# Decoder block on one core: the shared expert ahead of the routed experts, the residual on VectorE, the expert ranking right behind the router

## The chip, the cores and the metric

The kernel runs on one core of a Trainium2 chip. The metric is the device time of one execution in microseconds (us); the median of three runs before the change is 930.93 us (929.96 to 931.77). All arithmetic is on 32-bit floats; where TensorE multiplies, a number is mostly split into a high and a low part of the type `fp32r`, and three products (high by high, low by high, high by low) are added up.

## What is computed

One decoder layer for 256 tokens of width 1024. Attention and a gated recurrence give `x1`, the residual stream after the first LayerNorm. What follows is what the change touches, cut from the reference:

```
h = x1.reshape(B * S, D)                      # 256 x 1024
idx, gate = route(h, w_router, bias)          # 8 of 64 experts per token
y_moe = routed_experts(h, idx, gate, ...)     # each expert: silu(xb Wg) * (xb Wu), then Wd; ff 256
      + swiglu(h, shared_w_gate, shared_w_up, shared_w_down)   # the shared expert, every token
ple = sigmoid(x1 @ ple_gate_w) * (p @ ple_proj_w)              # the "embedding" term
x = layer_norm(ALPHA * x1 + y_moe + ple)
```

Each expert has 3 MB of weights, so the 64 of them have 192 MB, and the shared expert has 3 MB more.

## The kernel before

A helper `mm` (line 105) records nearly every matmul, so tiles tell more than lines: `pj`, `ah`, `mix` belong to the part before `x1`, `acc` is the sum of the output (four banks, two halves of tokens by two halves of columns), `t` and `g` are the banks of the expert part. `load` (line 83) issues every weight transfer on the queue of SP, in order.

**The ring.** Weights arrive in slots of 128 x 2048 floats (1 MB each), which the function `slot` hands out in turn. There are 17 of them while `x1` is made; the buffer of `x1` joins when `x1` is no longer wanted, and two more when the buffers of the embedding's stage are closed, which makes 20. A transfer into a slot waits until the last reader of what was in it is done, and because SP issues in order, every transfer behind it waits too.

**The stage between `x1` and the experts** (380 to 424 us). TensorE transposes `x1` into `x1h` and `x1l` (high and low part, `xT` for short), forms the router's logits, and multiplies `x1` with the embedding's gate: `dense` (two calls, `gated[0]` and `gated[1]`) takes 8 chunks of weights each, splits a chunk on ScalarE (line 119) and VectorE or GpSimd (line 120) and issues 6 matmuls for it. Beside it VectorE selects the 8 experts of every token and makes `posm`, the place of a token among its expert's tokens. `add_emb` (line 806) splits the gated embedding and adds it to `acc` with an identity matrix.

**The experts.** `units` lists 13 units, each with two passes. In ten of them a pass takes 2 experts with up to 64 tokens each; in three (places 2, 7 and 9 of the list, `SMALL_AT`) a pass takes 4 experts with up to 32 tokens each. The function `experts` issues a pass: the gate and up matmuls (`g<-raw,xe`), the activation, the down matmuls (`g<-raw,hT`), the scatter into `acc`; between them it calls the generators in `steps`, which gather the tokens of the next unit. A pass of 2 experts uses 6 MB of weights, one of 4 uses 12 MB, with nearly the same TensorE time.

**The order of the experts.** The first 8 experts (`FIXED`) have their place in the program. From the ninth on the experts are sorted by their number of tokens: `rank` counts, sorts, rewrites `posm` and `gates2`, and leaves the experts' numbers in `ids` (in the tile `cst`, line 737). SP reads a number with `TENSOR_LOAD` (line 815) before it issues that expert's loads, and the number of rounds (tile `rounds`, line 753) likewise. `rank` is a generator whose four pieces are spread over the first two passes of the experts.

**The shared expert** is a generator too, `shared`, and its pieces are spread over units 4 to 6 (`SHARED_AT` 6). It adds `ALPHA * x1` to `acc` with 12 matmuls by a scaled identity matrix, transposes the split `x1` again (32 transposes of 128 x 128), takes its 3 MB of weights in program order behind the experts' loads, issues 48 matmuls for gate and up and 24 for down, and keeps its splits in ring slots.

The last unit's end is the second LayerNorm (`last_norm`) and the store of the result.

Of the kernel before, what the change touches and what calls it, by code (L numbers as in the profile page):

```python
# [33 lines left out]
SHARED_AT = 6  # L34
FIXED, SMALL, SMALL_AT = 8, 24, (2, 7, 9)
# [3 lines left out]
SLOW, EMB_AT, GATHER_AT = ((0, 1), (0, 1, 2)), 4, (3, 4)  # L39
GU_AT = (5, 6)  # L40
# [18 lines left out]
def tile_block(ctx: ExitStack, tc: tile.TileContext, a, out: bass.AP):  # L59
# [560 lines left out]
    add_slots(pxx, 1, X_AT)  # L620
    lg = bank("t")[:NE, :S]

    def ev_ple(f):
        def ev(i, ps):
            o = emb[i][f]
            act.activation(ps, ps, AF.Sigmoid)
            late(dve.tensor_mul(o, o, ps))
        return ev

    gated = [dense([(raw(a["pleg"][2 * f + n]), 4) for n in range(2)], ev_ple(f),  # L630
                   [acc_bank() if f else bank("g") for _ in range(2)], SLOW[f]) for f in range(2)]
    for kt in range(KT):
        if kt == ROUTER_SPLIT:
            next(gated[0])
        ws = slice(NE * kt, NE * kt + NE)
        mm(lg, wrh[:, ws], x1h[:, kt], start=kt == 0, stop=False)
        mm(lg, wrh[:, ws], x1l[:, kt], start=False, stop=False)
        mm(lg, wrl[:, ws], x1h[:, kt], start=False, stop=kt == KT - 1)
# [55 lines left out]
    ids = cst[0:1, C_TRI:C_TRI + NE].bitcast(I32)  # L694

    def rank():


        t = slot()
        bigger, cnt, front, keys = (t[:, n:n + NE] for n in (0, 64, 128, 192))  # L700
        ranked = t[:, 256:384]
        pg, pgT = (t[:, n:n + 256].rearrange("p (i c) -> p i c", i=2) for n in (384, 640))
        em = t[:, 896:1024].rearrange("p (i e) -> p i e", i=2)
        rones, rcol, top, key = (t[:, n:n + 1] for n in range(1024, 1028))
# [93 lines left out]


    s, xe, steps = unit(0)  # L800
# [40 lines left out]
    w0, gu0 = expert_weights(0, 2), bank("g")  # L841
    for kt in range(KT):
        next(gated[1])
        if kt == EMB_AT:
            add_emb(0)
        if kt in GATHER_AT:
            next(steps)
        if kt in GU_AT:
            n = GU_AT.index(kt)
            gate_up(gu0, (2 * n, 2 * n + 1), xe, 0, w0)  # L850
    fixed["pe"] = False
    add_emb(1)
# [7 lines left out]

    def swiglu(h, ps):
        act.activation(h, ps[:, 0:256], AF.Sigmoid)  # L862
        for n in range(2):
            dve.tensor_mul(h, h, ps[:, 256 * n:256 * n + 256])  # L864
# [56 lines left out]
    def shared():  # L921


        keep = slot(F32R)
        ah, al = keep[:, 0:128], keep[:, 128:256]
        act.activation(ah, ident, CP, scale=ALPHA)
        dve.scalar_tensor_tensor(al, ident, ALPHA, ah.bitcast(F32), op0=OP.mult, op1=OP.subtract)
        for i in range(2):
            for f in range(2):
                for l, r in ((ah, xh), (ah, xl), (al, xh)):  # L930
                    mm(acc[i][f], l, r[:, i, 512 * f:512 * f + 512], start=False, stop=False)
                yield
        keep = slot(F32R)
        hth, htl = keep[:, 0:512], keep[:, 512:1024]
        xT = [slot(F32R).rearrange("p (k t) -> p k t", k=KT) for _ in range(2)]

        def split_into(hi, lo, c):
            act.activation(hi, c, CP)
            dve.tensor_sub(lo, c, hi.bitcast(F32))

        def splits(chunks):
            t = None
            for n, c in enumerate(chunks):
                if n % 2 == 0:
                    t = slot(F32R)
                hi, lo = (t[:, 512 * k:512 * k + 512] for k in (2 * (n % 2), 2 * (n % 2) + 1))
                split_into(hi, lo, c)
                yield hi, lo

        for x, t in zip((xh, xl), xT):  # L950
            for k2 in range(4):
                ps = bank("t", (128, 2, S))
                for k in range(2):
                    kt = 2 * k2 + k
                    for i in range(2):
                        transpose(ps[:, k, 128 * i:128 * i + 128], x[:, i, 128 * kt:128 * kt + 128].bitcast(F32))
                if k2 % 2:
                    act.activation(t[:, 2 * k2:2 * k2 + 2], ps, CP)
                else:
                    dve.tensor_copy(t[:, 2 * k2:2 * k2 + 2], ps)  # L960
                yield
        gu = [raw(a["shgu"][n], ordered=True) for n in range(2)]
        dn = raw(a["shd"], ordered=True)
        ps = [bank("g") for _ in range(2)]
        for kt, (whi, wlo) in enumerate(splits([r[:, 512 * k:512 * k + 512] for r in gu for k in range(4)])):
            for i in range(2):
                hi, lo = (t[:, kt, 128 * i:128 * i + 128] for t in xT)
                mm(ps[i], hi, whi, start=kt == 0, stop=False)
                mm(ps[i], lo, whi, start=False, stop=False)
                mm(ps[i], hi, wlo, start=False, stop=kt == KT - 1)  # L970
        hs = slot().rearrange("p (i c) -> p i c", i=2)
        for i in range(2):
            swiglu(hs[:, i, 0:256], ps[i])
        yield
        hT = bank("t", (128, 2, S))
        for i in range(2):
            for ft in range(2):
                transpose(hT[:, ft, 128 * i:128 * i + 128], hs[:, i, 128 * ft:128 * ft + 128])
        split_into(hth, htl, hT.rearrange("p f t -> p (f t)"))
        ws = splits([dn[:, 512 * k:512 * k + 512] for k in range(4)])  # L980
        for f in range(2):
            yield
            for ft in range(2):
                whi, wlo = next(ws)
                for i in range(2):
                    c = slice(256 * ft + 128 * i, 256 * ft + 128 * i + 128)
                    for l, r in ((hth, whi), (htl, whi), (hth, wlo)):
                        mm(acc[i][f], l[:, c], r, start=False, stop=False)

# [11 lines left out]
    ranking = rank()  # L1001
    for q, (r0, ne) in enumerate(units):
        if q + 1 < len(units):
            if q == 1:
                for _ in ranking:
                    pass
            first = steps
            nxt, xnxt, steps = unit(q + 1)
            fill = (none, steps, steps, none), (none, steps, steps, none)
            if q == SHARED_AT - 2:  # L1010
                sh = shared()
                fill = ((sh, steps, steps, sh),) * 2
            if q == SHARED_AT - 1:
                fill = ((zip(sh, sh), steps, steps, zip(sh, sh)),) * 2
            if q == 0:
                fill = ((list(first) for _ in (0,)), steps, steps, ranking), (ranking, steps, steps, ranking)
# [5 lines left out]
        for pr in range(2):  # L1022
            r = r0 + ne * pr
            last = q + 1 == len(units) and pr == 1
            if q == SHARED_AT and pr == 0:
                for _ in rest:
                    pass
                rest = ()
                next(sh)
                chained = (next(sh) for _ in (next(steps, None),))  # L1030
                fill = (sh, steps, chained, sh), fill[1]
# [214 lines left out]
```

## Time and profile before

| | us |
|---|---|
| median of three runs | 930.93 |
| the profiled execution's own time | 932.01 |
| its span, first to last instruction | 930.2 |
| TensorE busy in it | 873.6 (94%) |
| bytes moved by DMA | 270.84 MB, mean 291 GB/s |

The span is what the trace shows; the execution has 1.8 us more around it. Busy time of TensorE is modelled: matmuls overlap, so a high share does not mean that TensorE was what the end waited for. The chain of waits, followed back from the last instruction, tells that. DMA share 1.00 means that all 16 DMA engines were busy.

### The profile page before, as it was taken

The numbers are of one execution on the slowest core, as the hardware profiler recorded it, in microseconds if no ns is written. First come the engines' busy times: TensorE is split into PE (matmuls) and PEld (weight loads), VectorE is DVE, ScalarE is ACT, GpSimd is POOL, SyncE is SP. The second block draws the span as 40 slices with busy tenths as digits, with TensorE's granted clock in tenths as the row PEclk, the third lists the DMA queues.
The fourth block names the chain that finished last, engine by engine and source line by source line (L and its number), as shares of the span: only waits on it lengthen the run. The fifth ranks groups of instructions, "written<-read, shape, count | busy, mean of one in ns | idle before, by whom it ended". The sixth has DMA issues, their size and how long they took to land.

```text
span 930.2 us, 14043 instructions
## 1 busy us (share of the span) xinstructions
PE 873.6 (94%) x5244; PEld 575.7 (62%) x5244; DVE 381.3 (41%) x808; ACT 328.8 (35%) x657; POOL 169.9 (18%) x219
## 2 busy tenths in 40 slices
PE   9999999999999999799998999999987987799993
PEld 7899897878799998665543444546532432244431
DVE  5555555777966566852211221243110111011216
ACT  6444454576665455542221221242110211011221
POOL 1025354734200002440210110120100110101001
PEclk9999999999999999899999999999998999899997
DMA  9953342534246974547399999984999999999971
GB/s 340 421 219 105 123 136 91 183 106 164 81 170 218 395 304 169 186 168 292 154 422 420 420 420 421 421 352 186 421 421 421 419 421 422 420 421 421 412 315 47
DMA packets 42047, 270.84 MB, mean 291 GB/s; under 512 B 5060, under 2 KB 5188, under 8 KB 12280
## 3 DMA queue, kind: packets, MB, share of 16 engines
q1 hardware_dynamic: 41624, 269.20, 72.7%
q8 instruction: 42, 0.69, 0.3%
q10 hardware_dynamic: 288, 0.52, 0.1%
q14 instruction: 29, 0.24, 0.1%
q0 software_dynamic: 64, 0.20, 0.1%
HBM read 268.85 MB, written 1.05 MB: 290 GB/s over the span
## 4 chain that ended last, share of the span: by engine, by line
PE 65%; DMA 27%; DVE 5%; issue 1%; ACT 1%; SPq 1%; DVEq 0%; ACTq 0%
DMA raw<-in_exp_dram 27%; PE pj L105 25%; PE g L105 18%; PE acc L105 5%; PE t L105 5%; PE ah L105 4%; PE mix L474 2%; PE sc L105 1%; PE yp L105 1%; PE ap L383 1%; PE t L108 1%; PE pt L262 1%; DVE hr L367 1%; PE op L105 1%; SPq L83 0%
## 5 line engine op out<-in xcount | busy, mean ns | idle before, releaser
L105 PE MATMUL g<-raw,xe 128*64 128x512 f32 (+1 forms) x1024 | 212.0, 629 | 23.4 <-DMA raw<-in_exp_dram 23.4
L119 ACT ACTIVATE wh<-raw 128x512 fp32r<-128x512 f32 x213 | 132.3, 630 | 121.3 <-PE pj L105 88.1
L120 DVE TENSOR_TENSOR wl<-raw,wh 128x512 fp32r<-128x512 f32 x184 | 129.6, 715 | 90.5 <-ACT wh L119 69.5
L105 PEld LDWEIGHTS g<-raw,xe 128*64 128x64 f32 (+1 forms) x1024 | 61.5, 131 | 154.4 <-issue 110.4
L105 PE MATMUL pj<-xhi,wh 128*128 128x256 f32 x448 | 128.8, 288 | 0.2 <-DVE hq L368 0.2
L105 PE MATMUL pj<-xlo,wh 128*128 128x256 f32 x448 | 128.2, 286 | 0.0
L105 PE MATMUL pj<-xhi,wl 128*128 128x256 f32 x448 | 128.0, 286 | 0.0
L764 POOL TENSOR_SCALAR sel<-cst,posm 128x64 fp32r<-128x64 f32 (+1 forms) x120 | 48.2, 429 | 396.6 <-PE t L105 350.4
L864 DVE TENSOR_TENSOR h<-h,g 128x256 f32<-128x256 f32 x52 | 21.9, 420 | 222.8 <-ACT h L862 221.9
L105 PE MATMUL g<-raw,hT 128*64 128x512 f32 (+1 forms) x512 | 99.5, 598 | 4.3 <-DMA raw<-in_exp_dram 3.8
L862 ACT ACTIVATE h<-g 128x256 f32<-128x256 f32 x26 | 10.0, 384 | 222.5 <-PE g L105 222.5
L105 PEld LDWEIGHTS pj<-xhi,wh 128*128 128x128 f32 x448 | 85.5, 191 | 3.5 <-issue 1.9
L105 PEld LDWEIGHTS pj<-xhi,wl 128*128 128x128 f32 x448 | 85.5, 191 | 3.1 <-issue 2.7
L105 PEld LDWEIGHTS pj<-xlo,wh 128*128 128x128 f32 x448 | 85.5, 191 | 2.7 <-issue 2.4
L908 DVE SCALAR_TENSOR_TENSOR yl<-g,gsl,yh 128x512 fp32r<-128x512 f32 x52 | 39.0, 750 | 116.9 <-ACT yh L907 116.9
L105 PEld LDWEIGHTS g<-raw,hT 128*64 128x64 f32 (+1 forms) x512 | 27.8, 126 | 57.3 <-issue 43.8
L907 ACT ACTIVATE yh<-g,gsl 128x512 fp32r<-128x512 f32 x52 | 35.7, 687 | 75.5 <-PE g L105 75.5
L105 PE MATMUL t<-sel,xh 128*128 128x256 f32 x208 | 56.9, 306 | 1.3 <-DVE gsl L888 1.3
L105 PEld LDWEIGHTS t<-sel,xh 128*128 128x128 f32 x208 | 40.1, 193 | 23.0 <-issue 21.9
L778 ACT ACTIVATE xe<-t 128x512 f32<-128x512 f32 x52 | 31.1, 597 | 64.6 <-PE t L105 64.6
L105 PE MATMUL t<-sel,xl 128*128 128x256 f32 x208 | 52.5, 285 | 0.0
L120 POOL TENSOR_TENSOR wl<-raw,wh 128x512 fp32r<-128x512 f32 x29 | 38.4, 1333 | 60.0 <-ACT wh L119 43.6
(296 smaller groups left out, 1313.7 us busy)
## 6 DMA issues: line engine op xcount, KB each, us to landing
raw<-in_exp_dram SPq DMA_DIRECT2D x180, 1024.0 KB, 19.8
raw<-in_win_dram SPq DMA_DIRECT2D x40, 1024.0 KB, 5.0
raw<-in_exp_dram SPq DMA_DIRECT2D x24, 512.0 KB, 10.1
raw<-in_wab_dram SPq DMA_DIRECT2D x8, 768.0 KB, 5.3
raw<-in_wo_dram SPq DMA_DIRECT2D x4, 1024.0 KB, 8.1
raw<-in_pleg_dram SPq DMA_DIRECT2D x4, 1024.0 KB, 10.5
raw<-in_win_dram SPq DMA_DIRECT2D x8, 256.0 KB, 6.0
raw<-in_shgu_dram SPq DMA_DIRECT2D x2, 1024.0 KB, 19.9
```

Of the source, the lines that this page charges most:

```text
L105: pinned(pe.matmul(o, l, r, start=start, stop=stop))
L108: pinned(pe.transpose(o, t, ident))
L119: act.activation(hi, src, CP)
L120: (lo_engine or dve).tensor_sub(lo, src, hi.bitcast(F32))
L262: pe.transpose(pt[:, b], pr[:, 128 * b:128 * b + 128], ident)
L474: ins = pe.matmul(mix[i][f], l[:, ts], r[f], start=j == n == 0, stop=j == 7 and n == 2)
L764: by.tensor_scalar(s[:, i, w * e:w * e + w], iota[:, 0:w], pos_of(i)[:, e:e + 1], None, op0=OP.is_equal)
L778: act.activation(xe[k2], ps, CP)
L862: act.activation(h, ps[:, 0:256], AF.Sigmoid)
L864: dve.tensor_mul(h, h, ps[:, 256 * n:256 * n + 256])
L907: act.activation(yh, y, CP, scale=gsl)
L908: dve.scalar_tensor_tensor(yl, y, gsl, yh.bitcast(F32), op0=OP.mult, op1=OP.subtract)
```

## The change

- **Shared expert.** `shared` and its 32 transposes go. Its gate and up product is now a third call of `dense`, on the embedding's `x1h` and `x1l`, right behind `gated[1]`; its down product stands between the two halves of the first gate and up matmuls of the first experts. Its weights are asked for right behind the embedding's gate weights, before any expert's. Its splits use the buffers of the embedding's stage and no ring slots.
- **Residual.** `ALPHA * x1` is added to the embedding term on VectorE (4 instructions of 128 x 512), and so reaches `acc` with `add_emb`; the 12 matmuls go.
- **Ranking.** The four pieces of `rank` run between the chunks 1, 2, 3 and 5 of `gated[1]`; its scratch moves from a ring slot to buffers of its own.
- The gather of the first unit moves behind the shared gate and up product; the second small unit moves from place 7 to place 6 of the list.

```diff
-SHARED_AT = 6
-FIXED, SMALL, SMALL_AT = 8, 24, (2, 7, 9)
+FIXED, SMALL, SMALL_AT = 8, 24, (2, 6, 9)
-SLOW, EMB_AT, GATHER_AT = ((0, 1), (0, 1, 2)), 4, (3, 4)
-GU_AT = (5, 6)
+SLOW, RANK_AT = ((0, 1), (0, 1, 2), ()), (1, 2, 3, 5)
...
             late(dve.tensor_mul(o, o, ps))
+            late(dve.scalar_tensor_tensor(o, x1[:, i, 512 * f:512 * f + 512], ALPHA, o, op0=OP.mult, op1=OP.add))
...
+    sh_gu = [(raw(a["shgu"][n]), 4) for n in range(2)]
+    sh_dn = raw(a["shd"])
...
-    w0, gu0 = expert_weights(0, 2), bank("g")
+    w0 = expert_weights(0, 2)
+    ranking = rank()
     for kt in range(KT):
         next(gated[1])
-        if kt == EMB_AT:
+        if kt in RANK_AT:
+            next(ranking)
+    add_slots(pxx, 1, X_AT)
+    s, xe, steps = unit(0)
...
+    shared = dense(sh_gu, ev_shared, [bank("g") for _ in range(2)], SLOW[2])
+    for kt in range(KT):
+        if kt == 2:
             add_emb(0)
-        if kt in GATHER_AT:
-            next(steps)
-        if kt in GU_AT:
-            n = GU_AT.index(kt)
-            gate_up(gu0, (2 * n, 2 * n + 1), xe, 0, w0)
+            hs = ptg.tile([128, 2, S], F32, name="tg", bufs=4)
+        if kt == 4:
+            add_emb(1)
+        next(shared)
+    next(steps)
+    next(steps)
+    hT = bank("t", (128, 2, S))
...
+    act.activation(hth, hTf, CP)
+    late(dve.tensor_sub(htl, hTf, hth.bitcast(F32)))
+    gu0 = bank("g")
+    gate_up(gu0, range(2), xe, 0, w0)
+    for f in range(2):
+        for ft in range(2):
+            n = 2 * f + ft
+            whi, wlo = split(pbd, sh_dn[:, 512 * n:512 * n + 512], 512, "w2", W2)
+            for i in range(2):
+                c = slice(256 * ft + 128 * i, 256 * ft + 128 * i + 128)
+                for l, r in ((hth, whi), (htl, whi), (hth, wlo)):
+                    mm(acc[i][f], l[:, c], r, start=False, stop=False)
+    gate_up(gu0, range(2, 4), xe, 0, w0)
     fixed["pe"] = False
-    add_emb(1)
...
-    def shared():
...
```

How the instructions stand, at three places. First the queue of SP between the embedding's gate weights (`pleg`) and the first expert whose number is read (`cst`); `shgu` and `shd` are the shared expert's weights. Before:

```order
L83 DMA raw<-in_pleg_dram 128x2048 x4
L83 DMA raw<-in_exp_dram 128x2048 x10
L83 DMA xs<-in_rbias_dram 128x64
L83 DMA raw<-in_exp_dram 128x2048 x14
L815 TENSOR_LOAD cst
```

Now:

```order
L81 DMA raw<-in_pleg_dram 128x2048 x4
L81 DMA raw<-in_shgu_dram 128x2048 x2
L81 DMA raw<-in_exp_dram 128x2048
L81 DMA raw<-in_shd_dram 128x2048
L81 DMA raw<-in_exp_dram 128x2048 x7
L81 DMA xs<-in_rbias_dram 128x64
L81 DMA raw<-in_exp_dram 128x2048 x8
L819 TENSOR_LOAD cst
L819 ISA x2
L1029 TENSOR_LOAD rounds
L1029 ISA x2
L81 DMA raw<-in_exp_dram 128x2048 x2
```

The three shared chunks have moved ahead of the experts, and SP reads the numbers and the rounds behind 16 expert chunks instead of 24 (the `cst` pair stands four times in a row).

Second, TensorE where `rank` begins (its first piece has 4 small matmuls). Before, in the first pass of the experts:

```order
L105 MATMUL g<-raw,hT 64x512 x8
L105 MATMUL t<-raw 128x64 x2
L105 MATMUL t<-raw 64x1 x2
L105 MATMUL acc<-yh,sT 128x512
```

Now, in `gated[1]`, behind its second chunk:

```order
L103 MATMUL acc<-w2l,x1h 128x512
L103 MATMUL t<-xs,rcols 128x64 x2
L103 MATMUL t<-rcols,xs 64x1 x2
L103 MATMUL acc<-w2h,x1h 128x512
L103 MATMUL acc<-w2h,x1l 128x512
```

The first piece has moved ahead of six of the eight chunks of `gated[1]`, and all of `rank` ahead of the experts.

Third, TensorE from the end of the shared gate and up product to the shared down product, now (rows that repeat are left out; `tg` is the shared expert's activation, `w2h` and `w2l` its split weights):

```order
L103 MATMUL g<-w2l,x1h 128x512
L103 MATMUL t<-sel_4748,xh 128x256
...
L106 MATMUL t<-cst,tg 128x128 x4
L103 MATMUL g<-raw,xe 64x512 x4
L103 MATMUL acc<-w2h,tg 128x512 x2
L103 MATMUL acc<-w2l,tg 128x512
...
L103 MATMUL g<-raw,xe 64x512 x4
L103 MATMUL t<-sel_4748,xh 128x256
```

Before, the shared products stood in the sixth unit as rows like these:

```order
L105 MATMUL g<-raw 128x512 x48
L105 MATMUL t<-sel_6372,xh 128x256
L105 MATMUL g<-raw,xe 64x512 x8
L105 MATMUL t<-cst,raw 128x128 x4
L105 MATMUL acc<-raw 128x512 x12
```

What stood between passes of the experts now stands before the first one: 24 down matmuls lie between two groups of 4 gate and up matmuls.

## Rows read from the trace of the kernel before

**Rows 1.** The page: DMA share in 40 slices, and the chain that ended last.

```profile
DMA  9953342534246974547399999984999999999971
...
PE 65%; DMA 27%; DVE 5%; issue 1%; ACT 1%; SPq 1%; DVEq 0%; ACTq 0%
DMA raw<-in_exp_dram 27%; PE pj L105 25%; PE g L105 18%; PE acc L105 5%; PE t L105 5%; PE ah L105 4%; PE mix L474 2%; PE sc L105 1%; PE yp L105 1%; PE ap L383 1%; PE t L108 1%; PE pt L262 1%; DVE hr L367 1%; PE op L105 1%; SPq L83 0%
```

**Rows 2.** Busy time by stretch; the last three numbers are granted clock, DMA share, GB/s.

```profile
420.00:424.00 4.00, 4.00 (x21) 3.56 (x21) 0.07 (x1) 0.77 (x2) 0.00 (x0) 0.63 1.01 426
442.00:455.00 13.00, 13.00 (x72) 7.19 (x70) 4.50 (x14) 3.79 (x8) 0.88 (x3) 1.00 0.00 2
...
606.00:642.00 36.00, 34.71 (x176) 21.80 (x176) 13.80 (x27) 13.07 (x25) 5.32 (x16) 1.00 0.55 223
642.00:823.00 181.00, 155.82 (x846) 66.52 (x844) 27.30 (x67) 25.84 (x49) 15.26 (x40) 0.96 1.01 421
...
904.00:930.00 26.00, 10.23 (x46) 4.23 (x42) 14.29 (x36) 4.56 (x8) 4.18 (x3) 0.77 0.11 42
```

**Rows 3.** Waits on SP's queue, 380 to 930 us: total, times, longest.

```profile
SPq L815 <- DVE cst L737: 16.7, 1, 16.7
```

**Rows 4.** Issues on SP's queue, in order of time: start, length, what.

```profile
455.09 0.97 SPq L83 DMA_DIRECT2D raw<-in_exp_dram  x2
...
893.85 0.33 SPq L83 DMA_DIRECT2D raw<-in_exp_dram  x1
```

**Rows 5.** The page, DMA issues: KB each, median us to landing.

```profile
raw<-in_exp_dram SPq DMA_DIRECT2D x24, 512.0 KB, 10.1
```

**Rows 6.** The chain of waits, 528 to 570 us: start, length, what.

```profile
533.77 1.03 PE acc L105 x4
...
547.76 1.15 PE t L105 x8
...
549.25 1.03 PE acc L105 x4
...
565.78 1.03 PE acc L105 x4
```

**Rows 7.** The chain of waits, 383 to 430 us.

```profile
399.22 5.61 PE acc L105 x24
...
415.76 0.91 PE acc L105 x3
...
419.40 1.56 PE acc L105 x3
...
423.79 3.58 PE g L105 x16
```

**Rows 8.** VectorE in order of time, 399 to 406 us.

```profile
401.58 1.41 DVE L764 TENSOR_SCALAR sel<-cst,posm 128x64 fp32r<-128x64 f32 x8
...
403.52 0.21 DVE L706 TENSOR_SCALAR raw<-posm 128x128 f32<-128x128 f32 x1
```

**Rows 9.** Line 512 on VectorE: durations min/median/max in ns.

```profile
L512 DVE SCALAR_TENSOR_TENSOR x<-x,st,raw x4: 737/1242/1829, 376.4 to 380.5; 128x512 f32<-128x512 f32 x4
```

**Rows 10.** GpSimd's splits, 383 to 405 us: count, busy, mean ns, idle before.

```profile
L120 POOL TENSOR_TENSOR w2l<-raw,w2h 128x512 fp32r<-128x512 f32 x3 | 3.9, 1306 | 7.7 <-ACT w2h L119 7.7
```

**Rows 11.** TensorE in order of time: the 4 matmuls of `rank`'s first piece (8 records).

```profile
434.64 0.98 PE L105 MATMUL t<-raw 128*128 128x64 f32 x8
```

**Rows 12.** The page, costliest groups: busy us, mean ns, idle before.

```profile
L119 ACT ACTIVATE wh<-raw 128x512 fp32r<-128x512 f32 x213 | 132.3, 630 | 121.3 <-PE pj L105 88.1
L120 DVE TENSOR_TENSOR wl<-raw,wh 128x512 fp32r<-128x512 f32 x184 | 129.6, 715 | 90.5 <-ACT wh L119 69.5
...
L864 DVE TENSOR_TENSOR h<-h,g 128x256 f32<-128x256 f32 x52 | 21.9, 420 | 222.8 <-ACT h L862 221.9
...
L862 ACT ACTIVATE h<-g 128x256 f32<-128x256 f32 x26 | 10.0, 384 | 222.5 <-PE g L105 222.5
```

More of the change, by code (lines that the diff above doesn't have):

```diff
@@ L619, in tile_block @@
             (dve if i and f else pool).tensor_sub(xl[:, i, c], x1[:, i, c], xh[:, i, c].bitcast(F32))
-    add_slots(pxx, 1, X_AT)
     lg = bank("t")[:NE, :S]
@@ L694, in tile_block @@
     ids = cst[0:1, C_TRI:C_TRI + NE].bitcast(I32)
+    rcols = px.tile([128, 4], F32, name="rcols")
     def rank():
[L699 to L704, printed above, removed]
+        t, t2 = (px2.tile([128, 512], F32, name="xs", bufs=2) for _ in range(2))
+        pg, pgT = (v[:, 0:256].rearrange("p (i c) -> p i c", i=2) for v in (t, t2))
+        em, ranked = t[:, 256:384].rearrange("p (i e) -> p i e", i=2), t2[:, 256:384]
+        (bigger, keys), (cnt, front) = ((v[:, 384:448], v[:, 448:512]) for v in (t, t2))
+        rones, rcol, top, key = (rcols[:, n:n + 1] for n in range(4))
         pool.memset(rones, 1.0)
@@ L797, in unit, with swiglu @@
         return s, xe, gather(new_xe, bank, s, 4, xe)
-    s, xe, steps = unit(0)
+    def swiglu(h, ps):
+        act.activation(h, ps[:, 0:256], AF.Sigmoid)
+        for n in range(2):
+            dve.tensor_mul(h, h, ps[:, 256 * n:256 * n + 256])
     acc = [[None, None], [None, None]]
@@ L839, in gate_up, with ev_shared @@
                    w[e][kt // 4][:, 512 * (kt % 4):512 * (kt % 4) + 512], start=kt == 0, stop=kt == KT - 1)
-    w0, gu0 = expert_weights(0, 2), bank("g")
+    w0 = expert_weights(0, 2)
+    ranking = rank()
     for kt in range(KT):
         next(gated[1])
-        if kt == EMB_AT:
-            add_emb(0)
-        if kt in GATHER_AT:
-            next(steps)
-        if kt in GU_AT:
-            n = GU_AT.index(kt)
-            gate_up(gu0, (2 * n, 2 * n + 1), xe, 0, w0)
+        if kt in RANK_AT:
+            next(ranking)
+    add_slots(pxx, 1, X_AT)
+    s, xe, steps = unit(0)
+    hs = None
+    def ev_shared(i, ps):
+        swiglu(hs[:, i], ps)
+    shared = dense(sh_gu, ev_shared, [bank("g") for _ in range(2)], SLOW[2])
+    for kt in range(KT):
+        if kt == 2:
+            add_emb(0)
+            hs = ptg.tile([128, 2, S], F32, name="tg", bufs=4)
[7 more added lines that the diff above has]
+        for ft in range(2):
+            transpose(hT[:, ft, 128 * i:128 * i + 128], hs[:, i, 128 * ft:128 * ft + 128])
+    hth, htl = (ptg.tile([128, 512], F32R, name="tg", bufs=4) for _ in range(2))
+    hTf = hT.rearrange("p f t -> p (f t)")
+    act.activation(hth, hTf, CP)
[3 more added lines that the diff above has]
+    for f in range(2):
+        for ft in range(2):
+            n = 2 * f + ft
+            whi, wlo = split(pbd, sh_dn[:, 512 * n:512 * n + 512], 512, "w2", W2)
+            for i in range(2):
+                c = slice(256 * ft + 128 * i, 256 * ft + 128 * i + 128)
+                for l, r in ((hth, whi), (htl, whi), (hth, wlo)):
+                    mm(acc[i][f], l[:, c], r, start=False, stop=False)
+    gate_up(gu0, range(2, 4), xe, 0, w0)
     fixed["pe"] = False
-    add_emb(1)
     bd.close()
@@ L858, in tile_block @@
     p3 = t2.enter_context(tc.tile_pool(name="p3", bufs=1, reuse_waits="tile"))
[L861 to L864, printed above, removed]
     def experts(pl, bk, xe, off, s, gates, w, add, before=(), steps=(iter(()),) * 4, begun=None):
@@ L919, in experts @@
         return scatter(1)
-    def shared():
[L924 to L988, printed above, removed]
@@ L1000, in tile_block @@
     fixed["pe"] = PE_FIXED
-    ranking = rank()
     for q, (r0, ne) in enumerate(units):
         if q + 1 < len(units):
-            if q == 1:
-                for _ in ranking:
-                    pass
             first = steps
             nxt, xnxt, steps = unit(q + 1)
[L1009 to L1014, printed above, removed]
+            fill = ((none, steps, steps, none),) * 2
             if q == 0:
-                fill = ((list(first) for _ in (0,)), steps, steps, ranking), (ranking, steps, steps, ranking)
+                fill = ((list(first) for _ in (0,)), steps, steps, none), fill[1]
         else:
@@ L1024, in tile_block @@
             last = q + 1 == len(units) and pr == 1
[L1025 to L1031, printed above, removed]
             w = expert_weights(r, ne, q + 1 == len(units)) if r else w0
```

## The prediction

> **What bounds the kernel now.** I read the page's chain of waits first. 27% of the span is DMA of expert weights, the largest single entry, although TensorE counts as busy for 94% [rows 1]. So the question is which stretch the DMA sets. The DMA's share by slices is full from about the middle to the end, with one dent [rows 1]. The busy times by stretch make it exact: no DMA at all from 442 to 455 us, 0.55 in 606 to 642, 1.01 at 421 GB/s in 642 to 823 [rows 2]. A chunk of 1 MB (1.049 million bytes) therefore takes 2.49 us, and nothing can make the stream denser.
>
> The third view is SP's waits: SP stood 16.7 us at the `TENSOR_LOAD` of the experts' numbers until `rank` had written them [rows 3]. The first expert chunk behind it was issued at 455.09, the last at 893.85 [rows 4], and it landed some 10.1 us later [rows 5], at 904.0. From 904 to the end at 930.2 come the last matmuls and the norm [rows 2]. So the end is: the time at which the stream restarts (455.1), plus the chunks that are then still to come, plus the hole at 606 to 642, plus a tail. At 455.1, 24 expert chunks have been issued, and 168 expert and 3 shared chunks are left, 171 in all. They take 904.0 - 455.1 = 448.9 us; 171 x 2.49 = 425.8, the hole is 36 x 0.45 = 16.2, and the remaining 7 us are start, half chunks and small losses, which I leave as they are.
>
> TensorE is close behind: a pass of 2 experts took 15.48 us (533.77 to 549.25 [rows 6]) and needs 6 chunks, 14.9 us of stream; a pass of 4 experts needs 29.9. Only the small units make TensorE wait, and they fix the end.
>
> **The change part by part.**
>
> *The hole goes.* The expert chunks behind the shared expert's waited for ring slots that its splits and transposes held. They use none now. Gain 16.2 us, if the stream has nothing else to wait for there.
>
> *The numbers come early.* All of `rank` now lies in `gated[1]`. SP reads numbers and rounds behind 16 expert chunks, and they are ready before the ring lets the next chunk in. The wait of 16.7 us goes; the ring is what is late next.
>
> *Three chunks ahead.* The shared chunks sit in 3 of 17 slots until the shared products have read them. Counted through the ring, the expert chunks that can be loaded before that are 16 in order and one that takes `x1`'s buffer: 17 instead of 24. The next one takes the slot of the shared down weights, and the stream can be steady from then on. Call that time S. Behind S come 192 - 17 = 175 chunks, 4 more than the 171: **+10.0 us**.
>
> *When S is.* TensorE begins `gated[1]` at 399.2 as before [rows 7]. A matmul there takes 5.61/24 = 0.234 us [rows 7], a chunk of 6 takes 1.40.
> - 8 chunks of `gated[1]` and 8 of the shared gate and up product: 22.4 us.
> - `add_emb`: 8 matmuls, 1.9 us.
> - `rank`: 12 small matmuls at 0.98/4 = 0.245 [rows 11]: 2.9 us.
> - First wait: `rank`'s first matmul stands behind the second chunk, at 402.0. It needs VectorE's line 706, which ended at 403.7 before [rows 8]. In front of it 8 instructions of `sel` (1.41 us [rows 8]) go and two of the new residual instructions come. No row shows one; the nearest is line 512, the same operation and shape, with 0.74, 1.24 and 1.83 us as least, median and most [rows 9]. It ran beside GpSimd, as the first two residual instructions will (GpSimd's three splits of 1.3 us [rows 10]), so I take 1.1 each: 403.7 - 1.4 + 2.2 = 404.5, a wait of 2.5 us. Ends: 1.7 and 4.0.
> - Second wait: the embedding's second half needs TensorE, ScalarE, VectorE in turn. Before, TensorE stood at that place from 416.7 to 419.4, 2.7 us [rows 7]. Now four shared chunks cover it, but VectorE does two residual instructions and their splits more: I take 2.0. Ends: 0, and 9, if all of some 17 VectorE instructions of that shape took 1.24 instead of 0.72 [rows 9, 12].
>
> Sum 31.7: the shared gate and up product ends at 430.9. Then one activation 0.38, two pairs of products 4 x 0.42, one split 0.72 between them [rows 12]; 4 transposes at 0.14 [rows 6]: 434.3. Four gate and up matmuls (8 records, half of 3.58 [rows 7]) 1.8, six down matmuls 1.4, the last split 0.63 + 0.72 [rows 12]: **S = 438.9**, 16.2 us before 455.1.
>
> For the port: line 512 ran up to 1.83 us beside a GpSimd instruction that also reads two operands [rows 9, 10]. The Trainium skill says why ("SBUF — State Buffer", section "Who interferes with whom"): a VectorE instruction with two SBUF inputs comes in through a read port that GpSimd shares, and whichever starts first holds it, so moving the residual from TensorE to VectorE puts it in GpSimd's way. By that rule at its worst, both early ones cost 1.83, and S and the end come 1.5 us later.
>
> *The ring behind S.* 20 slots; the chunks of passes 3 to 6 go into slots that the first four passes free. A pass frees 6 in 15.48 us, the stream wants 14.9: it loses 0.55 a pass, 2.2 us in all. Ends: 0, and 4 x 1.6 = 6.4 with passes of 16.53 us (549.25 to 565.78 [rows 6]).
>
> *Costs at nothing.* The 32 transposes and 12 residual matmuls leave TensorE between 606 and 823 us, where the stream sets the pace [rows 2], so they give nothing; the 72 shared matmuls cost what is in S, and nothing later. The small unit's place (7 to 6) moves a wait of TensorE and no chunk: nothing, as long as the DMA is the bound; the last small unit and the three units behind it stand as before, so the tail stays.
>
> **Sum.** -16.2 (S) + 10.0 (4 chunks) - 16.2 (hole) + 2.2 (ring) = -20.2 us. The profiled execution took 932.0, so 911.8; the median of the runs shown is 1.1 lower, so **911 us**.
>
> **The rivals.**
> 1. *TensorE's pass becomes the bound.* If passes take 16.5 instead of 15.48, as they did with pieces of the shared expert between them [rows 6], the first four hold the stream (4 more us than counted) and the last six, behind the last small unit, end 6 x 1.05 = 6.3 later: 911 + 10 = 921. Against it: the pieces that made them longer are gone.
> 2. *No waits in front.* Both waits hidden (-4.5) and no loss in the ring (-2.2): 904. For it: where TensorE waited 2.7 us before [rows 7], four shared chunks now stand in between. Against: VectorE has four residual instructions and eight more splits to do in that stage.
> 3. *TensorE's clock falls in the front stage*, the one on the other side. After its wait of 2.7 us the granted clock was 0.63 of full in 420 to 424, a mix of the two levels 1.2 and 2.4 GHz [rows 2, 7]. If the two new waits put the stage at the lower level until its end, its 27.2 us of matmuls double, S is 466.1 and the end 911 + 27 = 938. From S = 459 on the change is a loss. Against it: in the trace the clock was back at 1.00 in 442 to 455 [rows 2], and the new waits are no longer than the old one. The Trainium skill ("TensorE: Matmul & The Clock Gate", section "What's actually happening") says that the lower clock is the default and sustained activity lifts it, which speaks against a whole stage at half speed; the rows bear that out.
> 4. *It doesn't do what it says*: numbers or slots still come late, and S falls at 459: 931, no change. The order of SP's queue speaks against it.
>
> **How the numbers follow.** Forecast (904 to 917) 0.74; rival 1 0.13; rival 2, below 904, 0.06; rival 3 0.05; rival 4 0.02. A measurement of this kernel can tell about 0.2% (1.9 us) from no change. So faster 0.93, same 0.02, slower 0.05. The range for 8 in 10 takes the forecast, most of rival 1 and some of rival 2: 903 to 921. The ends fit the bounds: -6.7 with both waits and the ring at their least, +1.5 +7 at the waits' most.
>
> **What would show it.** Right: no `TENSOR_LOAD` wait on the numbers over a microsecond; DMA share near 1.0 from about 440 us to within 30 us of the end, without a dent; the stream's first steady chunk near 439; the last small unit ends some 20 us earlier. Wrong: DMA share below 0.95 between 440 and 500 (the ring), a shared product that ends past 436 (VectorE), a clock below 1.00 over more than 5 us of the front stage, or a new hole.

## The result, and the profile after

The changed kernel took **909.62 us** (median of 4 runs, 909.14 to 911.18); the kernel before took 930.44 (929.41 to 931.77) beside it. The ratio is 0.9778, with a 95% interval of 0.976 to 0.9796: faster by 20.8 us, where the prediction said 911 us in a range of 903 to 921. The profiled execution took 909.14 us, with a span of 907.4. The profiled execution of before was 1.6 us longer than its median, so differences of spans come out about 2 us larger than those of medians.

The page of the changed kernel, DMA share in 40 slices and the chain that ended last, to hold against [rows 1]:

```profile
DMA  8953433443334988344799999999999999999971
...
PE 76%; DMA 16%; DVE 5%; issue 1%; ACT 1%; SPq 0%; DVEq 0%
```

The dent in the second half is gone, and DMA's part of the chain fell from 27% to 16%. Busy time by stretch makes it exact. The columns are those of [rows 2]: stretch, busy time of PE, PEld, DVE, ACT and POOL, then granted clock, DMA share and GB/s.

```profile
442.00:455.00 13.00, 12.36 (x66) 6.01 (x66) 3.08 (x7) 3.91 (x8) 0.00 (x0) 1.00 1.01 422
455.00:500.00 45.00, 45.00 (x231) 21.14 (x228) 8.50 (x20) 9.04 (x18) 8.63 (x24) 1.00 0.99 399
500.00:550.00 50.00, 49.68 (x344) 22.40 (x345) 10.61 (x26) 10.34 (x19) 3.32 (x8) 1.00 1.01 417
606.00:642.00 36.00, 34.51 (x216) 15.59 (x213) 6.47 (x16) 7.04 (x13) 3.32 (x8) 1.00 1.01 421
```

From 442 to 455, where nothing moved before, the stream is full, and from 606 to 642 the share rose from 0.55 to 1.01. Only 455 to 500 is a little thin: 399 instead of 421 GB/s, which is 45 x (1 - 399/421) = 2.3 us of stream. The granted clock is 1.00 in each of these stretches.

Waits on SP's queue, 380 to 930 us, and three issues on it in order of time (start, length, what), to hold against [rows 3, 4]:

```profile
SPq L81 <- DVE w2l L118: 33.9, 5, 9.7
...
SPq L819 <- DVE w2l L811: 0.3, 1, 0.3
SPq L1029 <- DVE w2l L118: 0.2, 1, 0.2
```

```profile
425.47 0.33 SPq L81 DMA_DIRECT2D raw<-in_exp_dram  x1
...
435.55 0.33 SPq L81 DMA_DIRECT2D raw<-in_exp_dram  x1
...
871.19 0.33 SPq L81 DMA_DIRECT2D raw<-in_exp_dram  x1
```

The wait of 16.7 us for the experts' numbers is now 0.3 us, and the one for the rounds 0.2. The first of the three issues is the 17th expert chunk, the second the 18th. Between them SP waits 9.7 us, until line 118 on VectorE has made the last split of the shared down weights and so freed their slot; then the stream is steady. So S = 435.55 us in this execution. The last chunk is issued at 871.19 instead of 893.85, 22.7 us earlier.

**Where the 22.7 us come from**, by the prediction's own sum: S is 19.5 us before the old restart at 455.09; 175 chunks are left instead of 171, +10.0; the hole is gone, -16.2. That makes -25.7. The 3.0 us that are missing lie in the first 60 us behind the restart, where the kernel before was a little thin too, but less (405 GB/s in 455 to 500). The same 60 us of both, before and after:

```profile
455.09:515.09 60.00, 57.32 (x354) 24.88 (x350) 10.66 (x27) 10.17 (x20) 7.67 (x22) 0.97 1.00 410
```

```profile
435.55:495.55 60.00, 59.36 (x305) 29.68 (x304) 10.69 (x26) 12.13 (x23) 6.72 (x20) 1.00 0.98 389
```

They moved 410 and 389 GB/s, and 60 x 21/421 is 3.0 us. From the last issue to the end of the span it took 36.35 us before and takes 36.2 now.

### The profile page after: what moved, and what is told of

Its sections match the earlier page's. It is cut to its first block, busy times and chain, and to the rows that moved or that the text cites. A ratio compares the mean times of both kernels' runs of the same rounds, so it can differ in the third digit from the quotient of the medians.

```text
span 907.4 us, 13967 instructions
## 1 busy us (share of the span) xinstructions
PE 856.1 (94%) x5200; PEld 567.4 (63%) x5200; DVE 380.8 (42%) x807; ACT 327.3 (36%) x652; POOL 171.9 (19%) x219
## 4 chain that ended last, share of the span: by engine, by line
PE 76%; DMA 16%; DVE 5%; issue 1%; ACT 1%; SPq 0%; DVEq 0%
PE pj L103 26%; PE g L103 25%; DMA raw<-in_exp_dram 15%; PE t L103 6%; PE acc L103 6%; PE ah L103 4%; PE mix L472 2%; PE sc L103 2%; PE yp L103 1%; PE ap L381 1%; PE t L106 1%; PE pt L260 1%; DVE hr L365 1%; PE op L103 1%; DMA raw<-in_win_dram 0%
## 5 line engine op out<-in xcount | busy, mean ns | idle before, releaser
L103 PE MATMUL g<-raw,xe 128*64 128x512 f32 (+1 forms) x1024 | 203.9, 606 | 19.9 <-DMA raw<-in_exp_dram 19.9
L103 PEld LDWEIGHTS t<-sel,xh 128*128 128x128 f32 x208 | 39.2, 188 | 23.8 <-issue 22.7
## 6 DMA issues: line engine op xcount, KB each, us to landing
raw<-in_exp_dram SPq DMA_DIRECT2D x180, 1024.0 KB, 19.8
```

What stands on the lines that cost most here:

```text
L103: pinned(pe.matmul(o, l, r, start=start, stop=stop))
```

## Experiments

Each kernel ran on one chip beside the kernel before; the ratio is to that, with its 95% interval. The restart is the first expert chunk behind the numbers (in the changed kernel's family, where the ring is later than the numbers, the 18th chunk); it and the hole are read from one profiled execution. The hole is the stretch times the missing share.

| | us | ratio to before | restart | hole, us |
|---|---|---|---|---|
| changed kernel | 909.62 | 0.9778 (0.976 to 0.9796) | 435.55 | 0 |
| 1 ranking alone | 918.62 | 0.9883 (0.9866 to 0.9899) | 436.21 | 19.8 |
| 2 shared expert and residual alone | 922.43 | 0.9924 (0.9908 to 0.9941) | 468.45 | 0 |
| 3 ten us more in front | 918.92 | 0.9885 (0.9868 to 0.9901) | 445.62 | 0 |
| 4 residual late, on TensorE | 907.25 | 0.9762 (0.9746 to 0.9778) | 432.51 | 0 |
| 5 ranking, shared expert packed | 911.73 | 0.9797 (0.9779 to 0.9815) | 438.08 | 10.9 |
| 6 ranking one chunk later | 909.57 | 0.9777 (0.9761 to 0.9793) | 433.88 | 0 |
| 7 last small unit at 11 | 907.60 | 0.9752 (0.9734 to 0.977) | 436.95 | 0 |
| 8 second small unit at 7 | 910.61 | 0.979 (0.9773 to 0.9807) | 437.25 | 0 |
| 9 ranking, shared behind place 6 | 900.73 | 0.9679 (0.9663 to 0.9694) | 438.03 | 4.2 |
| 10 ranking, shared behind place 2 | 913.38 | 0.9815 (0.98 to 0.9831) | 437.54 | 9.5 |

### 1 and 2: each half of the change alone

Experiment 1 is the kernel before with `rank` moved (shown against before), experiment 2 the changed kernel with it moved back (shown against the change).

```diff
     for kt in range(KT):
         next(gated[1])
         if kt == EMB_AT:
             add_emb(0)
-        if kt in GATHER_AT:
-            next(steps)
...
+        if kt in RANK_AT:
+            next(ranking)
+    s, xe, steps = unit(0)
```

```diff
-    ranking = rank()
     for kt in range(KT):
         next(gated[1])
-        if kt in RANK_AT:
-            next(ranking)
...
+    ranking = rank()
     for q, (r0, ne) in enumerate(units):
         if q + 1 < len(units):
+            if q == 1:
+                for _ in ranking:
+                    pass
```

> The kernel before with the ranking alone moved: its four pieces run between chunks 1, 2, 3 and 5 of the embedding's second gate product, with scratch of its own; the first unit's gather and its first 16 gate and up matmuls stand behind that. The shared expert stays spread over units 4 to 6, the residual stays on TensorE. Stream theory (the end is the restart of the expert stream plus what is left of it plus the hole): SP no longer waits 16.7 us for the numbers, the stream restarts 13 to 16 us earlier with the same chunks left, and the hole at 606 to 642 us stays: 914 to 917 us. Rival A (behind the numbers the ring or TensorE is late by as much): 928 to 931 us. Rival B (the ring and the hole shift, so the earlier stream only waits longer at the hole): between 920 and 928, with a hole longer than 16 us.

> The changed kernel with the ranking put back into the first two passes of the experts (scratch in a ring slot, as before). Shared expert and residual stay in front. Stream theory: SP is held again at the experts' numbers, now until about 470 us, since the passes start 15 us later than before; by then 24 expert chunks are loaded and 168 are left, and there is no hole: 930.4 + 15 (restart) - 16.2 (hole) - 7.5 (3 shared chunks already in) = 922 us, give or take 4, with a wait of 25 to 35 us on the numbers. Rival (the shared expert's place alone brings the whole gain): 908 to 912 us.

The ranking alone gives 11 us, the rest alone 7, both together 21. Busy time by stretch in experiment 1, and its waits on SP's queue from 590 to 642 us:

```profile
442.00:500.00 58.00, 57.84 (x358) 26.78 (x360) 12.16 (x29) 12.53 (x23) 8.63 (x24) 1.00 1.01 421
500.00:606.00 106.00, 105.84 (x572) 51.44 (x565) 22.32 (x53) 22.61 (x43) 11.18 (x28) 1.00 1.01 420
606.00:642.00 36.00, 34.35 (x170) 21.25 (x170) 13.42 (x26) 12.07 (x24) 4.10 (x13) 1.00 0.45 181
```

```profile
SPq L83 <- PE g L105: 24.8, 3, 13.6
SPq L83 <- DVE raw L963: 17.7, 2, 17.5
```

The stream restarts 18.9 us earlier (436.21 against 455.09), but the hole grows from 16.2 to 36 x 0.55 = 19.8 us: 3.6 us of the gain go there, as rival B of that run had it in kind, though not in size. What SP waits for in the hole is work of the shared expert in ring slots: copies of the transposed `x1` (line 963) and, for the 13.6 us, the matmuls of its gate and up product. The end is just above the forecast.

Experiment 2, the wait on the numbers and the first issue behind it:

```profile
SPq L819 <- DVE cst L737: 16.8, 1, 16.8
```

```profile
468.45 0.36 SPq L81 DMA_DIRECT2D raw<-in_exp_dram  x1
```

The restart is 13.4 us later than before, 168 chunks instead of 171 are left (-7.5), and the hole is gone (-16.2): -10.3, and the last chunk was issued at 883.63 instead of 893.85, 10.2 earlier. The sum holds in a kernel that moves its terms the other way. The wait was forecast at 25 to 35 us and is 16.8, because SP came to it later, behind loads that waited for slots.

### 3: does the end hang on S?

```diff
         next(shared)
+    dummy = bank("t")
+    for _ in range(43):
+        mm(dummy, one, xh[:, 0, 0:512])
     next(steps)
```

> The changed kernel with 43 more matmuls of 128x512 (into a bank that nobody reads, some 10 us) between the shared gate and up product and the first gather. Stream theory (the stream's steady start S hangs on TensorE's work in front, and the end on S): S at 445.5 instead of 435.5 and the end 10 us later, 919 to 921 us. Rival (the front has slack, for instance because the ring behind S loses less when the passes start later against the stream): at most 3 us later, 909 to 913.

```profile
445.62 0.33 SPq L81 DMA_DIRECT2D raw<-in_exp_dram  x1
```

S moves by 10.07 us and the end by 9.3 (by the ratios 9.9). So there is no slack at this place in front: within the noise, the 10 us that TensorE spends more before S are 10 us at the end.

### 4 and 6: what the residual on VectorE costs

Experiment 4 takes the four residual instructions off VectorE and puts the 12 matmuls into the fifth unit; experiment 6 leaves them and shifts `rank`.

```diff
-            late(dve.scalar_tensor_tensor(o, x1[:, i, 512 * f:512 * f + 512], ALPHA, o, op0=OP.mult, op1=OP.add))
...
+            if q == 4:
+                res = residual()
+                fill = ((res, steps, steps, res),) * 2
```

```diff
-SLOW, RANK_AT = ((0, 1), (0, 1, 2), ()), (1, 2, 3, 5)
+SLOW, RANK_AT = ((0, 1), (0, 1, 2), ()), (2, 3, 4, 6)
```

> The changed kernel without the four residual instructions on VectorE; the 12 residual matmuls by a scaled identity stand in the fifth unit instead, as they did before. If VectorE's residual sits on the path to S (TensorE's wait of 1.75 us before the ranking), the two early instructions of 0.68 to 0.76 us leave it and the end comes 0.7 to 1.5 us sooner: 908 to 909 us. Rival A (the residual is off the path): no difference, 909.3 to 910. Rival B (the matmuls or the ring slot that the identity takes hold up the stream): 2 to 4 us later, 911.5 to 914.

> The changed kernel with the four pieces of the ranking one chunk of the gate product later each (behind chunks 2, 3, 4 and 6). If TensorE's wait of 1.75 us before the ranking is on the path to S: S and the end 1.4 to 1.8 us sooner, ratio to the changed kernel 0.998 to 0.9985, as without the residual on VectorE. Rival A (VectorE is the path, TensorE only meets it elsewhere): no difference within 0.5 us. Rival B (the numbers come too late for SP): a wait on the numbers over 3 us and up to 2 us later.

TensorE's wait in the changed kernel, in order of time, and the four residual instructions (durations min/median/max in ns):

```profile
401.73 0.39 PE L103 MATMUL acc<-w2l,x1h 128*128 128x512 f32 x1
403.88 0.63 PE L103 MATMUL t<-xs,rcols 128*128 128x64 f32 x4 [1.75 <-DVE xs L706]
```

```profile
L625 DVE SCALAR_TENSOR_TENSOR tg<-x,tg x4: 679/682/762, 400.4 to 419.2; 128x512 f32<-128x512 f32 x4
```

In experiment 4 TensorE waits for nothing between 396 and 436 us, and S is 432.51. Of the 3.0 us by which that is earlier, 1.75 are the wait; 1.1 are the clock of this one execution (last section). The medians of the ratios say 1.5 us, at the rim of their intervals. So the residual on VectorE costs about what the wait is long, which the intervals do not separate from nothing, and no cost of the 12 matmuls can be seen where the stream sets the pace. In this kernel SP does stand at the numbers (4.0 us) and at the rounds (7.5 us): `x1`'s buffer comes free earlier, while in the changed kernel SP stood 8.1 us until the residual had read it. All this lies before S, which hangs on the slot of the shared down weights here too.

Experiment 6 is inconclusive. In its profile the wait is 0.4 us and a second one of 0.4 appears, before a matmul of the shared product that waits for a split on VectorE:

```profile
PE g L103 <- DVE w2l L118: 0.4, 1, 0.4
PE t L103 <- DVE xs L706: 0.4, 1, 0.4
```

S is 1.7 us earlier there, but 1.0 of that is the clock (the router's 12 matmuls took 1.47 us there and 2.49 in the changed kernel, see the last section), and the profiled execution was the fastest of the five. That leaves 0.7, where the waits are 0.95 us shorter, and the median is that of the changed kernel. Neither a gain of this size nor zero can be excluded.

### 7 and 8: the small units' places

```diff
-FIXED, SMALL, SMALL_AT = 8, 24, (2, 6, 9)
+FIXED, SMALL, SMALL_AT = 8, 24, (2, 6, 11)
```

```diff
-FIXED, SMALL, SMALL_AT = 8, 24, (2, 6, 9)
+FIXED, SMALL, SMALL_AT = 8, 24, (2, 7, 9)
```

> The changed kernel with the last small unit at place 11 of the list instead of 9, so that two passes of two experts follow it instead of six. Stream theory with TensorE 0.55 us a pass slower than the stream: TensorE falls 4 passes x 0.55 = 2.2 us less behind the stream after the last small unit, 1 to 2.5 us sooner. Rival A (the last landing sets the end, whatever stands before it): no difference within 0.5 us. Rival B (up to the last small unit TensorE falls behind by more than the ring holds): later by 2 us or more.

> The changed kernel with the second small unit back at place 7 of the list. Stream theory: the order moves a wait of TensorE and no chunk, so no difference, within 0.5 us. Rival (TensorE gets two passes more before its wait, so slots come free later and the stream loses 0.55 us a pass): 1 to 2 us later.

With the last small unit at 11 the ratio is 0.0026 lower, 2.4 us, though the two intervals still overlap. Its last chunk is issued at 873.34 and its span ends at 906.7: 33.4 us from the last issue to the end, 2.8 less than the 36.2 of the changed kernel. That fits TensorE falling less behind. The place of the second small unit (7 instead of 6) gives 0.0012 more, 1.1 us, within the intervals: none can be told.

### 5, 9 and 10: is the shared expert's place in front needed at all?

By the sum, the place in front costs 10.0 us for four chunks that could have been loaded. Experiment 5 keeps experiment 1's order and packs the shared expert into 8 ring slots instead of 14. Experiments 9 and 10 let no slot be held long: the transposes stand in a small unit, the products behind it, and the split of the activation takes its slot late. All three are shown against experiment 1.

```diff
-        keep = slot(F32R)
-        hth, htl = keep[:, 0:512], keep[:, 512:1024]
+        hth, htl = (keep[:, n:n + 512] for n in (256, 768))
+        pairs = slot(F32R)
...
-                if n % 2 == 0:
-                    t = slot(F32R)
-                hi, lo = (t[:, 512 * k:512 * k + 512] for k in (2 * (n % 2), 2 * (n % 2) + 1))
+                hi, lo = (pairs[:, 512 * k:512 * k + 512] for k in (2 * (n % 2), 2 * (n % 2) + 1))
```

```diff
-SHARED_AT = 6
-FIXED, SMALL, SMALL_AT = 8, 24, (2, 7, 9)
+SHARED_AT = 7
+FIXED, SMALL, SMALL_AT = 8, 24, (2, 6, 11)
...
-            if q == SHARED_AT - 2:
+            if q == SHARED_AT - 1:
                 sh = shared()
                 fill = ((sh, steps, steps, sh),) * 2
-            if q == SHARED_AT - 1:
-                fill = ((zip(sh, sh), steps, steps, zip(sh, sh)),) * 2
+            if q == SHARED_AT + 1:
+                res = residual()
+                fill = ((res, steps, steps, res),) * 2
```

Experiment 10 has `SHARED_AT` 3 and the small units at 2, 7 and 9.

> The kernel with the ranking alone moved, and its late shared expert packed tighter: the splits of its weights go through one ring slot instead of six and the identity shares the slot of the activation's split, so that shared expert and residual take 8 slots of the ring (3 of them weights) instead of 14. Stream theory: the stream restarts at 436 us with 171 chunks left as before, and the hole of about 20 us at 606 to 642 shrinks by half to all of it: 899 to 909 us, 9 to 20 less than the ranking alone, and, if the hole is gone, below the changed kernel by up to 10 us, which is what the four chunks not yet loaded cost that one. Rival A (the hole is TensorE's, not the slots': 30 us of shared work between passes hold the loads anyway): 916 to 919 us. Rival B (one slot for all splits makes TensorE wait between chunks): a longer hole, over 920.

> The kernel with the ranking alone moved, and its late shared expert rearranged so that no ring slot is held for long: the transposes of x1 lie in the small unit at place 6, where TensorE waits for the stream, the shared products in the first pass behind it, the split of the activation takes its slot only when it is needed, the residual follows in the unit behind with a slot of its own; small units at places 2, 6 and 11. Stream theory (end = restart 436 us + 171 chunks of 2.49 us, no hole, 7 us of small losses, tail 24 to 26 us): 895 to 901 us, 9 to 14 less than the changed kernel, since 24 instead of 20 chunks are in before the restart. Rival A (long-held slots are not what makes the hole, any shared expert between passes does): a hole of over 8 us, 907 to 914. Rival B (without the hole TensorE's own work is the bound): DMA share below 1 in the last 100 us and 902 to 907.

> The same with the shared products behind the first small unit (place 2; small units at 2, 7 and 9). Stream theory: after the first small unit TensorE is still 4 to 9 chunks behind the stream, and 25 us of shared work more make it fall behind by all that the ring holds, so the stream stalls by some us there: 897 to 904, 1 to 4 more than with the place behind the second small unit. Rival (the place does not matter once no slot is held long): within 1 us of it after 2 us for the last small unit's place.

Busy time by stretch in experiment 5, 606 to 680 us:

```profile
606.00:642.00 36.00, 35.47 (x178) 22.62 (x178) 14.97 (x29) 13.91 (x25) 5.36 (x16) 1.00 0.75 311
642.00:680.00 38.00, 37.84 (x234) 17.75 (x230) 7.97 (x18) 7.84 (x14) 3.33 (x8) 1.00 0.95 390
```

Its longest wait on SP's queue from 500 to 680 us:

```profile
SPq L83 <- PE acc L105: 13.7, 1, 13.7
```

Experiment 9, 442 to 823 us:

```profile
442.00:500.00 58.00, 57.84 (x352) 27.35 (x352) 12.62 (x30) 12.91 (x24) 8.63 (x24) 1.00 1.01 421
...
606.00:642.00 36.00, 29.21 (x192) 11.49 (x190) 6.12 (x13) 5.49 (x10) 0.00 (x0) 1.00 1.01 420
642.00:680.00 38.00, 34.11 (x189) 19.98 (x190) 13.87 (x28) 12.21 (x24) 3.32 (x8) 1.00 0.89 360
680.00:823.00 143.00, 141.87 (x752) 68.10 (x748) 28.04 (x65) 28.46 (x53) 15.27 (x40) 1.00 1.01 421
```

Its issue of the last chunk:

```profile
867.29 0.33 SPq L83 DMA_DIRECT2D raw<-in_exp_dram  x1
```

Experiment 10, 500 to 550 us, and its waits on SP's queue from 500 to 680:

```profile
500.00:550.00 50.00, 48.45 (x289) 28.34 (x282) 17.64 (x36) 15.43 (x30) 3.31 (x8) 1.00 0.81 330
```

```profile
SPq L83 <- DVE raw L940: 11.8, 1, 11.8
SPq L83 <- DMA raw<-in_shgu_dram: 8.7, 1, 8.7
```

Packing alone shrinks the hole from 19.8 to 36 x 0.25 + 38 x 0.05 = 10.9 us, and the end comes 6.9 us sooner (8.0 by the ratios): less than the forecast of 899 to 909, and against both rivals. What SP still waited for, 13.7 us at once, is a slot that the shared down matmuls into `acc` read last; two such slots (the split activation's and the weights' splits') are taken well before the down matmuls that end their use. Experiment 9 leaves 38 x 0.11 = 4.2 us of hole. It takes **900.73 us: 8.9 less than the changed kernel**, and the best of all. By the sum, against the changed kernel: 4 chunks less behind the restart -10.0, the restart itself +2.5, the hole +4.2, the thin stretch that is now full -2.3, and from the last issue to the end 32.0 us instead of 36.2 (899.3 - 867.29), -4.2: together -9.8, where the spans differ by 8.1. Part of this is not the shared expert's place: experiment 9 has its last small unit at 11, as experiment 7 has, and against that one it is 6.9 us shorter. So, with experiment 2, the ranking in front is needed and the shared expert in front is not.

Experiment 10 is the miss: 913.38 where 897 to 904 was expected. The same code one small unit earlier has a hole of 50 x 0.19 = 9.5 us, 5.3 more than experiment 9; in 455 to 500 its stream is thin (399 GB/s instead of 420), 2.2 us; and from the last issue (875.00) to the end it takes 36.5 us instead of 32.0, with the last small unit at 9. Together 12.0 of the 12.2 us between the spans. SP's long waits there end with the landing of the shared gate and up weights and with a split of shared weights (line 940). Both experiments hold each slot as briefly, so brief holding alone does not make the hole small; the place counts too. TensorE's longest entry of waits in experiment 9, 600 to 690 us:

```profile
PE g L105 <- DMA raw<-in_exp_dram: 9.3, 7, 1.5
```

In experiment 10 TensorE waits for no expert weights at all from 460 to 560 us. So ahead of the shared products the stream is what is late at place 6, and TensorE at place 2, where the shared work in slots then holds up chunks that the stream already wants. By how many chunks TensorE is behind there was not measured.

## Why the prediction was right, point by point

- **The numbers come early**: right. 16.7 us became 0.3, and the ring was late next, as said. Experiments 1 and 2 show the wait going and coming with `rank` alone.
- **The hole goes**: right, 0.55 became 1.01; it comes back when the shared expert does (experiment 1).
- **17 chunks before S, 175 behind it**: right to the chunk, and the four chunks' 10.0 us fit: the sum of experiment 9, which does not pay them, closes to 1.7 us with them. No run moved them alone.
- **S = 438.9**: it was 435.55. The step that failed is "I take 2.0" for the second wait. There was none: the four shared chunks covered the splits of the embedding's second half completely, and TensorE went from 403.88 to 438.4 without stopping, as the chain of waits shows below. The first wait was 1.75 instead of 2.5, because a residual instruction took 0.68 us (0.76 at most) and not 1.1: the row taken for it, line 512, was a poor stand-in. Another 0.8 us is in the eight microseconds behind the shared product, which took 7.2; 0.2 went the other way in between. And 435.55 has luck in it: in experiments 7 and 8, with the same program up to there, S was 436.95 and 437.25, because the clock fell behind the first wait (rival 3).

```profile
403.88 0.95 PE t L103 x8
404.83 1.58 PE acc L103 x6
...
419.05 2.83 PE g L103 x12
421.88 0.93 PE acc L103 x4
422.81 5.58 PE g L103 x24
428.38 1.91 PE t L103 x16
430.29 0.61 PE t L106 x4
430.90 1.87 PE g L103 x8
432.77 5.67 PE acc L103 x24
```

- **Ring, +2.2**: 3.0, all of it in the first 60 us behind S. The mechanism is in doubt: in experiment 1, with passes of the same length, the first 60 us behind the restart are full (421 GB/s), so passes that are slower than the stream do not make this loss by themselves. Passes took the forecast's 15.48 us (543.31 to 558.79 in the chain of waits), so rival 1 fell.
- **Sum**: S 3.3 us too late, the ring 0.8 too little, together 2.5: the forecast of 911.8 for a profiled execution stands against 909.14. The medians differ by 20.8, near the forecast's 20.2, because the profiled execution of before was 1.6 us longer than its median, which took most of these 2.5 back. That the two differences lie within 0.6 us is luck.
- **Rival 2** (no waits, no ring loss) was half right: one of its two waits was hidden, the ring's loss was not. **Rival 3** came in small, though not in the changed kernel's own profile. Granted clock in 404 to 412, behind the wait of 1.75 us, in the changed kernel and in experiment 7:

```profile
404.00:412.00 8.00, 8.00 (x45) 6.16 (x45) 4.38 (x14) 2.80 (x5) 1.08 (x3) 1.00 0.32 125
```

```profile
404.00:412.00 8.00, 8.00 (x37) 5.90 (x37) 3.56 (x13) 2.16 (x4) 0.96 (x3) 0.79 0.33 125
```

  In experiment 7 it was at the lower level, 0.50, from 406 to 408. Experiments 3 and 8 have the same wait and 0.79 there too; in experiments 4 and 6, where TensorE does not wait or waits 0.4 us, it is 1.00. Such a fall costs about 1.5 us of S (the matmuls from 404.7 to 410.0 in experiment 7 took 1.5 us longer than in the changed kernel), not the 27 that rival 3 asked for.
- **The small unit's place, nothing**: not refuted by experiment 8; and **the tail stays**: right, 36.35 and 36.2 us from the last issue.

## What to carry to other kernels

Where a stream of transfers sets the end, write the end as restart plus what is left of the stream plus its holes plus the tail, and cost each part of a change by which of these it moves; against the kernel before this sum gave the last issue within 3.0 us in the changed kernel and in experiments 1, 2, 5 and 9, which moved its terms in opposite directions, and missed experiment 10 by 5.4. In a ring that is filled in order, scratch that sits in slots stalls everything behind it: fewer slots (experiment 5) made the hole smaller, and so did brief holding together with a place where the consumer waits for the stream anyway (experiment 9). Which of these two counts more is not shown; brief holding at another place was not enough (experiment 10). Moving work to the front is paid for in what could have been loaded meanwhile.

## What the runs showed of the hardware

**The clock rises at different moments in different executions.** Granted clock in the stretches 383 to 386 us, of the changed kernel and of experiment 4 (0.50 is the lower level, 1.2 GHz, and 1.00 the higher, 2.4 GHz):

```profile
383.00:384.00 1.00, 1.00 (x6) 1.00 (x5) 0.74 (x2) 0.74 (x3) 0.00 (x0) 0.50 0.87 344
384.00:385.00 1.00, 1.00 (x7) 1.00 (x6) 0.69 (x1) 1.00 (x4) 0.37 (x1) 0.50 0.97 410
385.00:386.00 1.00, 1.00 (x7) 0.96 (x6) 0.00 (x0) 1.00 (x3) 1.00 (x2) 0.67 1.00 418
```

```profile
383.00:384.00 1.00, 1.00 (x11) 1.00 (x10) 0.84 (x3) 1.00 (x3) 0.00 (x0) 1.00 0.83 319
```

The router's first 12 matmuls took 2.49 us at the lower level in the one and 1.38 at the higher in the other, with the same program up to there. This lies on the path to S, and so two executions can differ by a microsecond there. The fall behind TensorE's wait of 1.75 us, in three of the four profiles that have this wait, adds as much again. Effects of 1 to 2 us (experiments 4, 6, 7, 8) are therefore read from waits in the trace rather than from one execution's S.

**A VectorE instruction that takes four times as long as another of its shape.** Line 675 multiplies two tiles of 128x128; line 646 adds two of the same shape. VectorE and GpSimd in order of time:

```profile
391.14 0.29 DVE L646 TENSOR_TENSOR xs<-xs 128x128 f32<-128x128 f32 x1
...
398.00 1.27 DVE L675 TENSOR_TENSOR xs<-xs 128x128 f32<-128x128 f32 x1
...
400.36 0.76 DVE L625 SCALAR_TENSOR_TENSOR tg<-x,tg 128x512 f32<-128x512 f32 x1
```

```profile
396.54 2.58 POOL L118 TENSOR_TENSOR w2l<-raw,w2h 128x512 fp32r<-128x512 f32 x2 [7.66 <-ACT w2h L117]
399.29 1.29 POOL L118 TENSOR_TENSOR w2l<-raw,w2h 128x512 fp32r<-128x512 f32 x1 [0.17 <-ACT w2h L117]
```

The one of 1.27 us runs while GpSimd is in its first two splits and ends 0.15 us behind them; the residual instruction overlaps the third by 0.22 us and is 0.08 longer than the others. The Trainium skill ("SBUF — State Buffer", section "Who interferes with whom") says that a VectorE instruction with two SBUF inputs contends with a GpSimd instruction that reads SBUF, for a port that only one of them holds at a time. Line 675 agrees, and so does line 512 of the kernel before [rows 9]: of its four instructions the first two ran beside GpSimd and took 1.83 and 1.75 us, the last two came after it had ended, at 379.36, and took 0.74 each:

```profile
375.21 4.15 POOL L120 TENSOR_TENSOR w2l<-raw,w2h 128x512 fp32r<-128x512 f32 x3 [0.70 <-ACT w2h L119]
```

But it is not always VectorE that pays. The second and third residual instruction ran beside GpSimd too (line 708, 402.25 to 404.51, and line 764, 412.45 to 417.94) and took 0.68; line 708 took 2.26 us there, while in experiment 8 it took 0.69 and the residual beside it 0.77. So an idle GpSimd is not what made the forecast's 1.1 too long. Line 675 was 1.27 us in the kernel before too, so it is no part of the change, but it lies on the path to the first wait. In every profile here it ran beside GpSimd; it was not tried without.
